# Sums of squares for the FFN's norm: six vector adds become six accumulating transfers, and the norm's factor is taken one pair of projections later

## The chip, the cores and the metric

The kernel runs on one core of a Trainium2 chip. The metric is the device time of one launch in microseconds. A core has a matrix engine (TensorE, PE in the profile, with its weight loads as PEld), a vector engine (VectorE, DVE), an activation engine (ScalarE, ACT), a general engine (GpSimd, POOL) and a queue engine that issues most transfers (SyncE, SP). Each engine takes its own instructions in order; an instruction that must wait holds everything behind it on that engine. Work is handed from one engine to another, and from transfers to engines, by semaphores.

## The reference, cut to what matters

One layer of a streaming encoder on 640 tokens (512 of a prompt, 8 x 16 of samples), model width 1024, in float32. The last two steps of the layer are the ones that matter here:

```
y   = merged @ w_out
h   = x + y                                        # after the mixing part
hn  = h * rsqrt(mean(h*h) + eps) * norm_ffn_g      # RMSNorm over the 1024 channels
a   = silu(hn @ ffn_w_gate) * (hn @ ffn_w_up)      # width 2816
out = h + a @ ffn_w_down                           # then a last RMSNorm
```

The mean of squares is one number for each token. It is a factor that is the same for all channels, so the product with the gate's weights can be formed before it is known and scaled behind it.

## The kernel before, in words

Everything is kept transposed: channels on the 128 partitions, the 640 tokens along the row. A tensor of 1024 channels is four blocks of 256 channels, each a tile of 128 x 2 x 640 (two groups of 128 channels, `m` = 0 and 1). Matrix work goes in jobs, one for each block of 256 output channels, and two jobs make a pair. A job multiplies by seven products instead of eight (a scheme on 2 x 2 blocks whose operands are sums of weight blocks and sums of input blocks, named 1 to 7 in the code); each product is 12 matmuls of 128 x 320 columns for each job, as float32 is split into a high and a low part, `h` and `l`, and three of the four part products are taken. So a pair is 7 x 24 matmuls. The order of the products is 5, 1, 6, 3, 7, 2, 4 in the first pair of a stage (`FIRST`) and 5, 2, 1, 6, 3, 7, 4 in the others (`LATER`). After each product ACT or DVE takes the result out of PSUM (`ev_form`, `ev_add`).

Weights come through one-deep and two-deep staging tiles `wr`. Plain quarters are loaded from SP (L1048). Two of the seven weight operands need a sum of two quarters; there the second quarter is added by an accumulating transfer from POOL (L1051). ACT then casts the high part (`wh`, L90) and DVE subtracts it (`wl`, L85); some operands need one more DVE add first (L1033). This runs up to three products ahead of the matmuls, in four buffers (`HB`).

The stage around the change is the end of the output projection (four `out_job`s, two pairs) and the start of gate and up (eleven pairs, `gu_jobs(0)` to `gu_jobs(10)`: the gate's job and the up's job of one block). When a block j of `h` is complete, `done` writes it to memory (`hspill`), and `squares` squares it in place on ACT (L1561) and adds its two groups into `s`, which is the tile `rbc` (L1563 for block 0, L1566 for blocks 1 to 3: six adds of 128 x 640 on DVE). Blocks 0 and 1 do this at once; those of blocks 2 and 3 wait in the list `late`, and hooks in the first gate/up pair call them after its products 6 and 3. After product 7 of that pair `stats` runs: ten rows of matmul against a column of ones give the sums over partitions (`ptr`, L66), DVE and POOL turn them into the factor (L159, L161), `replicate` spreads it over the partitions (L177 on DVE, two matmuls into `ppv`, ACT copies back into `rbc`, L184). `swiglu(j)` is called when the up's job of pair j has its last product: it scales the gate by `rbc` (L1583), takes tanh on ACT (L1587), two more DVE instructions (L1588, L1589), and writes the result to memory (`aspill`, from SP). The finished blocks are read back (`raw<-aspill`) as input of the down projection while gate and up still run.

The code states a program order; a scheduler then places each engine's instructions, so that neighbours in the code may stand elsewhere in the queue. The tiles `h`, `g`, `u` and `th` share five buffers (`pair`) that go round: a new tile waits until the last reader of the old one is done.

Of the kernel before, what the change touches and what calls it, by code (L numbers as in the profile page):

```python
# [14 lines left out]
ALU = mybir.AluOpType  # L15
# [42 lines left out]
class Builder:  # L58
# [1169 lines left out]
    def post(self):  # L1228

        nc, a = self.nc, self.a  # L1230
# [17 lines left out]
        for j in range(4):  # L1248
            for m in range(2):
                r = raws[j][:, m, :]  # L1250
                nc.vector.scalar_tensor_tensor(r, r, self.g(G_MIX + 2 * j + m), self.rbc, op0=ALU.mult, op1=ALU.mult)
                t = (E, O)[m]
# [37 lines left out]
        for hf in range(2):  # L1290
# [28 lines left out]
            if hf:  # L1319

                h, l = P["w"][5] = flat("wh", F32R), flat("wl", F32R)
# [73 lines left out]
        pairs = [(x, self.LATER) for x in jobs]  # L1395

        def hook(job, p, f, when="post"):
            job.setdefault(when, {}).setdefault(p, []).append(f)
# [55 lines left out]
        def add(jobs):  # L1454
            for i in range(0, len(jobs), 2):
                pairs.append((jobs[i:i + 2], self.LATER if i else self.FIRST))
# [77 lines left out]
        s = self.rbc  # L1534
        late = []

        def out_job(j):
            st = {}

            def load():  # L1540
                if j == 0:
                    sh["t"] = self.ap.tile([128, 4, 2, T], F32, tag="acc", bufs=1, name="hg")
                st["h"] = pair("h")
                self.dma(st["h"], a["xT"][256 * j:256 * j + 256, :].rearrange("(m p) t -> p m t", p=128))
                st["ev"] = self.ev_add(st["h"], done)

            def done(q):
                m, n = q
                h = st["h"]
                ns = slice(HN * n, HN * n + HN)  # L1550
                nc.scalar.activation(sh["t"][:, j, m, ns], h[:, m, ns], AF.Copy, scale=self.g(G_FFN + 2 * j + m))
                if q == (1, 0):
                    self.dma(self.hdram[j], h)
                    if j < 2:
                        squares()
                    else:
                        late.append(squares)

            def squares():
                h = st["h"]  # L1560
                nc.scalar.activation(h, h, AF.Square)  # L1561
                if j == 0:
                    nc.vector.tensor_tensor(s, h[:, 0, :], h[:, 1, :], op=ALU.add)  # L1563
                else:
                    for m in range(2):
                        nc.vector.tensor_tensor(s, s, h[:, m, :], op=ALU.add)  # L1566
            return {"ap": a["w_o"][j], "xc": xo, "ev": lambda p, ps: st["ev"](p, ps), "load": load}

        out = [out_job(j) for j in range(4)]
# [11 lines left out]
        def swiglu(j, g, u):  # L1581
            rb = self.rbc[:, None, :].broadcast_to([128, 2, T])
            nc.vector.tensor_tensor(g, g, rb, op=ALU.mult)  # L1583
            if j >= 8:
                nc.vector.tensor_tensor(u, u, rb, op=ALU.mult)
            th = pair("th")
            nc.scalar.activation(th, g, AF.Tanh, scale=0.5)  # L1587
            nc.vector.scalar_tensor_tensor(g, th, 1.0, g, op0=ALU.add, op1=ALU.mult)  # L1588
            nc.vector.tensor_tensor(g, g, u, op=ALU.mult)  # L1589
            self.dma(self.adram[j], g)  # L1590

        def gu_jobs(j):
            st = {}

            def done(name):
                def f(t, q):
                    st[name] = t
                    if name == "u" and q == (1, 0):
                        swiglu(j, st["g"], t)
                return f  # L1600
            return [{"ap": a["w_fg"][j], "xc": xf, "ev": self.ev_form(lambda: pair("g"), done("g"))},
                    {"ap": a["w_fu"][j], "xc": xf, "ev": self.ev_form(lambda: pair("u"), done("u"))}]

        n0 = len(pairs)
        add([x for j in range(NF // 2) for x in gu_jobs(j)])
        for p in (6, 3):
            hook(pairs[n0][0][1], p, lambda: late.pop(0)())
        hook(pairs[n0][0][1], 7, stats)

        ys = {}  # L1610

# [36 lines left out]
        for j in range(3):  # L1648
            self.dma(raw[:, j], self.adram[8 + j])
            for m in range(2):  # L1650
                h, l = places.pop(0)
# [181 lines left out]
```

## Time and profile before

| | us |
|---|---|
| median of 3 runs | 1284.82 (1284.57 to 1285.51) |
| the profiled execution | 1284.68 |
| its span, first to last instruction | 1282.6 |
| PE busy | 1249.0 (97%) |
| DVE busy | 930.9 (73%) |
| ACT busy | 653.2 (51%) |
| POOL busy | 162.8 (13%) |

The profile is of one execution; 2.1 us of its time lie outside the span. PE is busy 97% of the span, so its idle times are few and each can be looked up with the instruction that ended it. The stage of the change lies between about 820 and 890 us: block 0 of `h` is squared at 825 us, the factor's matmuls stand at 868 us, and the second gate/up pair begins at 877 us. Times in rows are microseconds from the span's start, and an instruction's row gives its start, its duration, its engine, its line and its tiles.

### The profile page before, as it was taken

The numbers are of one execution on the slowest core, as the hardware profiler recorded it, in microseconds if no ns is written. First come the engines' busy times: TensorE is split into PE (matmuls) and PEld (weight loads), VectorE is DVE, ScalarE is ACT, GpSimd is POOL, SyncE is SP. The second block draws the span as 40 slices with busy tenths as digits, with TensorE's granted clock in tenths as the row PEclk, the third lists the DMA queues.
The fourth block names the chain that finished last, engine by engine and source line by source line (L and its number), as shares of the span: only waits on it lengthen the run. The fifth ranks groups of instructions, "written<-read, shape, count | busy, mean of one in ns | idle before, by whom it ended". The sixth has DMA issues, their size and how long they took to land. (4 is left out here: it accounts for less than half of the span.)

```text
span 1282.6 us, 21826 instructions
## 1 busy us (share of the span) xinstructions
PE 1249.0 (97%) x8464; PEld 1197.9 (93%) x8464; DVE 930.9 (73%) x1467; ACT 653.2 (51%) x1135; POOL 162.8 (13%) x190
## 2 busy tenths in 40 slices
PE   7999999999999999999999899999999999999997
PEld 6999899998889779999999899999999999999997
DVE  7844465327777948777779877897777667899975
ACT  6733342326665568645565523574444444656334
POOL 5300001000001401211111001112111211111001
PEclk9999999999999999999999999999999999999998
DMA  7874533353434925876888996668766766697444
GB/s 246 263 275 172 188 111 109 120 169 98 117 103 139 319 40 155 229 198 173 264 267 253 295 338 192 174 174 229 192 185 186 186 166 171 183 248 203 128 133 132
DMA packets 107415, 241.21 MB, mean 188 GB/s; under 512 B 11120, under 2 KB 21232, under 8 KB 107312
## 3 DMA queue, kind: packets, MB, share of 16 engines
q1 hardware_dynamic: 89680, 204.43, 48.3%
q0 software_dynamic: 17360, 35.14, 14.4%
q8 instruction: 66, 1.08, 0.3%
q14 instruction: 37, 0.30, 0.1%
q10 hardware_dynamic: 272, 0.26, 0.1%
HBM read 204.50 MB, written 34.24 MB: 186 GB/s over the span
## 5 line engine op out<-in xcount | busy, mean ns | idle before, releaser
L85 DVE TENSOR_TENSOR wl<-wr,wh 128x1024 fp32r<-128x1024 f32 (+5 forms) x325 | 332.5, 1035 | 142.9 <-ACT wh L90 140.8
L90 ACT CAST wh<-wr 128x1024 fp32r<-128x1024 f32 (+5 forms) x325 | 281.7, 881 | 237.0 <-PE psX L1111 82.7
L1111 PE MATMUL psX<-Eh,wl 128*128 128x320 f32 x304 | 95.9, 315 | 3.3 <-DVE g L1137 3.3
L1111 PE MATMUL psX<-El,wh 128*128 128x320 f32 x304 | 94.5, 311 | 0.0
L1111 PE MATMUL psX<-Eh,wh 128*128 128x320 f32 x304 | 94.5, 311 | 0.0
L1033 DVE TENSOR_TENSOR wr<-wr 128x1024 f32<-128x1024 f32 x52 | 63.5, 1220 | 0.3
L1111 PEld LDWEIGHTS psX<-Eh,wl 128*128 128x128 f32 x304 | 57.7, 190 | 4.5 <-DVE g L1137 3.8
L1111 PE MATMUL psX<-c,wh 128*128 128x320 f32 x272 | 60.1, 309 | 0.0
L1111 PEld LDWEIGHTS psX<-Eh,wh 128*128 128x128 f32 x304 | 57.9, 190 | 0.2 <-issue 0.2
L1111 PEld LDWEIGHTS psX<-El,wh 128*128 128x128 f32 x304 | 57.7, 190 | 0.0
L66 PE MATMUL psb<-xh,wl 128*128 128x320 f32 x224 | 53.4, 319 | 0.0
L196 ACT ACTIVATE P<-psc,nb 128x256 f32<-128x256 f32 (+4 forms) x60 | 30.3, 506 | 44.0 <-DVE nb L190 38.5
L66 PE MATMUL psb<-xl,wh 128*128 128x320 f32 x224 | 51.5, 311 | 0.0
L66 PE MATMUL psb<-xh,wh 128*128 128x320 f32 x224 | 50.8, 308 | 0.0
L1051 POOL DMA_DIRECT2D wr<-in_w_fg x22 | 19.6, 892 | 243.3 <-DVE wl L85 122.7
L1111 PE MATMUL psZ<-Oh,wl 128*128 128x320 f32 x152 | 47.4, 312 | 1.0 <-DVE wl L85 1.0
L190 DVE TENSOR_REDUCE nb<-psc 128x1 f32<-128x256 f32 (+4 forms) x60 | 27.0, 456 | 27.6 <-PE psc L66 27.0
L1111 PE MATMUL psZ<-Ol,wh 128*128 128x320 f32 x152 | 47.0, 309 | 0.0
L1111 PE MATMUL psZ<-Oh,wh 128*128 128x320 f32 x152 | 46.9, 309 | 0.0
L1111 PEld LDWEIGHTS psX<-c,wh 128*128 128x128 f32 x272 | 45.5, 188 | 0.0
L1111 PE MATMUL psX<-c,wl 128*128 128x320 f32 x136 | 42.2, 310 | 0.6 <-DVE h L1151 0.5
L66 PEld LDWEIGHTS psb<-xh,wl 128*128 128x128 f32 x224 | 36.2, 188 | 5.9 <-issue 5.8
(507 smaller groups left out, 4068.5 us busy)
## 6 DMA issues: line engine op xcount, KB each, us to landing
wr<-in_w_fg SPq DMA_DIRECT2D x55, 256.0 KB, 3.7
wr<-in_w_fu SPq DMA_DIRECT2D x55, 256.0 KB, 4.4
wr<-in_w_fd SPq DMA_DIRECT2D x40, 256.0 KB, 4.2
cache<-in_ck SPq DMA_DIRECT2D x8, 1024.0 KB, 8.5
cache<-in_cv SPq DMA_DIRECT2D x8, 1024.0 KB, 7.7
aspill<-g SPq DMA_DIRECT2D x11, 640.0 KB, 3.2
raw<-aspill SPq DMA_DIRECT2D x11, 640.0 KB, 7.6
wr<-in_w_ft SPq DMA_DIRECT2D x16, 384.0 KB, 3.0
```

Source lines behind the costliest of these rows:

```text
L66: i = self.nc.tensor.matmul(out, lhsT=l, rhs=r, start=start, stop=stop)
L85: self.keep(self.nc.vector.tensor_tensor(out, a, b, op=ALU.subtract))
L90: self.keep(self.nc.scalar.copy(h, src))
L190: nc.vector.reduce_max(nb, ps, axis=AX.X, negate=True)
L196: nc.scalar.activation(P, ps, AF.Exp, bias=nb, scale=scale, accum_out=se)
L1033: nc.vector.tensor_tensor(src, src, r[{6: "11", 3: "12"}[p]], op=ALU.add)
L1051: self.nc.gpsimd.dma_start(out=t[:, 512 * k:512 * k + 512], in_=part(job, self.QUARTERS.index("22" if q == "s1" else "11")), accum_op=ALU.add)
L1111: self.nc.tensor.matmul(ps, lhsT=lw[:, ws], rhs=rx[:, k, :], start=first and k == 0 and i == 0, stop=last and k == 3 and i == 2, skip_grou ...
```

## The change

Three things differ. The six DVE adds at L1566 become six transfers from POOL that add `h` into `rbc` in place (`accum_op`); block 0 keeps its DVE add. The squares of blocks 2 and 3 are called after products 5 and 1 of the first gate/up pair instead of 6 and 3. The factor (`stats`) is taken after product 5 of the gate's job of the second pair instead of after product 7 of the first, and `swiglu(0)` is put off until after product 5 of the up's job of the second pair.

```diff
                 else:
                     for m in range(2):
-                        nc.vector.tensor_tensor(s, s, h[:, m, :], op=ALU.add)
+                        nc.gpsimd.dma_start(out=s, in_=h[:, m, :], accum_op=ALU.add)
...
                     if name == "u" and q == (1, 0):
-                        swiglu(j, st["g"], t)
+                        if j:
+                            swiglu(j, st["g"], t)
+                        else:
+                            late.append(lambda: swiglu(0, st["g"], t))
...
         n0 = len(pairs)
         add([x for j in range(NF // 2) for x in gu_jobs(j)])
-        for p in (6, 3):
+        for p in (5, 1):
             hook(pairs[n0][0][1], p, lambda: late.pop(0)())
-        hook(pairs[n0][0][1], 7, stats)
+        hook(pairs[n0 + 1][0][0], 5, stats)
+        hook(pairs[n0 + 1][0][1], 5, lambda: late.pop(0)())
```

The first place to look at is POOL's queue from the weights of the first gate/up pair on. In the names, `wr_9053` is a staging tile of the first gate/up pair, `wr_9516` (now `wr_9492`) the tile for product 5 of the third pair and `wr_9295` (now `wr_9298`) that for product 7 of the second; `fg` and `fu` are the gate's and the up's weights. Before:

```order
L1051 DMA wr_9053<-in_w_fg 128x512
L1051 DMA wr_9053<-in_w_fu 128x512
L1051 DMA wr_9516<-in_w_fg 128x512
L1051 DMA wr_9516<-in_w_fu 128x512
L1051 DMA wr_9295<-in_w_fg 128x512
L1051 DMA wr_9295<-in_w_fu 128x512
L161 TENSOR_TENSOR rstd_9438<-ms_9436,mhalf_73 128x5
```

And now, where `h_8873` is block 2 and `h_8889` is block 3:

```order
L1051 DMA wr_9053<-in_w_fg 128x512
L1051 DMA wr_9053<-in_w_fu 128x512
L1566 DMA rbc_74<-h_8873 128x640 x2
L1566 DMA rbc_74<-h_8889 128x640
L1051 DMA wr_9492<-in_w_fg 128x512
L1051 DMA wr_9492<-in_w_fu 128x512
L1051 DMA wr_9298<-in_w_fg 128x512
L1051 DMA wr_9298<-in_w_fu 128x512
L1566 DMA rbc_74<-h_8889 128x640
L161 TENSOR_TENSOR rstd_9528<-ms_9526,mhalf_73 128x5
```

Three of the four adds of blocks 2 and 3 stand ahead of the four weight transfers, and the last stands behind them. Since all write `rbc`, each add waits on POOL until the one ahead of it has landed. The two adds of block 1 stand further up, ahead of the tile for product 5 of the second pair.

The second place is PE's queue at the factor's matmuls (`ptr`). Before, they stand in the first pair, inside the gate's product 2 (`psZ_9452`):

```order
L1111 MATMUL psZ_9452<-Ol_4956,wh_9328 128x320
L1111 MATMUL psZ_9452<-Oh_4955,wl_9329 128x320
L1111 MATMUL psZ_9452<-Oh_4955,wh_9328 128x320
L66 MATMUL ptr_9430<-ones_71,rbc_74 128x1 x5
L1111 MATMUL psZ_9452<-Ol_4956,wh_9328 128x320
L1111 MATMUL psZ_9452<-Oh_4955,wl_9329 128x320
```

Now they stand between the two jobs of the second pair's product 5 (`psY_9505` is the gate's, `psY_9538` the up's):

```order
L1111 MATMUL psY_9505<-c6h_4957,wl_9401 128x320
L1111 MATMUL psY_9505<-c6h_4957,wh_9400 128x320
L1111 MATMUL psY_9505<-c6l_4958,wh_9400 128x320
L66 MATMUL ptr_9520<-ones_71,rbc_74 128x1 x5
L1111 MATMUL psY_9538<-c6h_4957,wl_9401 128x320
L1111 MATMUL psY_9538<-c6h_4957,wh_9400 128x320
```

They have moved back by the rest of the first pair and by 12 matmuls of the second, and they now wait for the landing of the last add, where before they waited for DVE.

On ACT both late squares now stand ahead of the cast for product 3 of the first pair, where before the second of them stood four casts further down. On DVE the six adds are gone; `swiglu(0)` stays in the second pair, some instructions later.

## Rows read from the trace of the kernel before

**Rows 1.** The page's first part: busy time of each engine.
```profile
PE 1249.0 (97%) x8464; PEld 1197.9 (93%) x8464; DVE 930.9 (73%) x1467; ACT 653.2 (51%) x1135; POOL 162.8 (13%) x190
```

**Rows 2.** Stretches of 10 us: PE, PEld, DVE, ACT, POOL busy; clock, DMA share, GB/s.
```profile
830.00:840.00 10.00, 9.59 (x66) 9.33 (x65) 9.64 (x16) 6.79 (x10) 3.36 (x4) 1.00 0.64 182
840.00:850.00 10.00, 9.82 (x67) 9.56 (x67) 10.00 (x13) 5.79 (x9) 0.17 (x1) 1.00 0.75 168
850.00:860.00 10.00, 8.17 (x54) 7.64 (x53) 9.88 (x14) 8.97 (x15) 0.00 (x0) 1.00 0.38 152
860.00:870.00 10.00, 9.77 (x69) 9.77 (x70) 9.01 (x14) 5.17 (x6) 3.94 (x5) 1.00 0.81 211
```

**Rows 3.** PE's timeline: matmuls behind idle time (in brackets: idle us and its releaser).
```profile
736.45 0.42 PE L1111 MATMUL psX<-Oh,wl 128*128 128x320 f32 x1 [3.07 <-DVE g L1137]
...
860.23 0.41 PE L1111 MATMUL psY<-c7h,wl 128*128 128x320 f32 x1 [1.52 <-DVE wl L85]
...
924.17 0.41 PE L1111 MATMUL psX<-Eh,wl 128*128 128x320 f32 x1 [1.47 <-DVE g L1137]
```

**Rows 4.** Line 1566: the six adds, ns min/median/max, first and last start.
```profile
L1566 DVE TENSOR_TENSOR rbc<-rbc,h x6: 817/821/825, 829.4 to 866.9; 128x640 f32<-128x640 f32 x6
```

**Rows 5.** ACT's timeline at the squares of blocks 2 and 3.
```profile
855.55 1.28 ACT L1561 ACTIVATE h<-h 128x1280 f32<-128x1280 f32 x1
...
857.67 2.95 ACT L90 CAST wh<-wr 128x1024 fp32r<-128x1024 f32 x3
...
861.78 1.29 ACT L1561 ACTIVATE h<-h 128x1280 f32<-128x1280 f32 x1
```

**Rows 6.** SP's timeline at the writes of blocks 2 and 3.
```profile
851.37 0.80 SPq L77 DMA_DIRECT2D hspill<-h  x2
```

**Rows 7.** The page's part 6, transfers: count, KB each, median us to landing.
```profile
hspill<-h SPq DMA_DIRECT2D x4, 640.0 KB, 4.1
```

**Rows 8.** POOL's timeline at the weights that stand behind the new adds.
```profile
863.87 0.86 POOL L1051 DMA_DIRECT2D wr<-in_w_fg  x1 [23.69 <-DMA wr<-in_w_fg]
...
867.24 1.14 POOL L1051 DMA_DIRECT2D wr<-in_w_fu  x1
```

**Rows 9.** Line 1051, all accumulating weight transfers of the trace: us to landing.
```profile
DMA to landing us min/median/max: 3.9/7.5/11.5
```

**Rows 10.** The same line, its four transfers between 860 and 875 us.
```profile
DMA to landing us min/median/max: 7.4/9.3/10.0
```

**Rows 11.** Stretches of 2 us, same columns as rows 2.
```profile
858.00:860.00 2.00, 0.71 (x5) 0.45 (x4) 2.00 (x3) 2.00 (x3) 0.00 (x0) 1.00 0.00 0
...
862.00:864.00 2.00, 2.00 (x15) 2.00 (x15) 2.00 (x3) 1.07 (x1) 0.13 (x1) 1.00 1.03 291
```

**Rows 12.** The chain of waits at the factor's matmuls: start, us, what.
```profile
868.28 1.01 PE ptr L66 x10
...
872.19 0.86 PE ppv L66 x2
...
873.93 0.37 PE ppv L66 x2
...
876.94 3.52 PE psY L1111 x24
```

**Rows 13.** The chain of waits from 955 to 985 us.
```profile
975.79 5.32 PE psX L1111 x24
```

**Rows 14.** Stretches around that place and behind the longest idle time of rows 3.
```profile
736.00:740.00 4.00, 3.55 (x24) 3.55 (x25) 4.00 (x6) 0.44 (x1) 0.00 (x0) 1.00 0.93 296
...
976.00:978.00 2.00, 2.00 (x13) 2.00 (x12) 1.97 (x4) 0.64 (x1) 0.00 (x0) 0.80 0.42 78
978.00:980.00 2.00, 2.00 (x9) 2.00 (x9) 2.00 (x2) 0.53 (x2) 0.00 (x0) 0.50 0.05 15
```

**Rows 15.** DVE's timeline at the first gate's scaling.
```profile
875.69 1.49 DVE L1583 TENSOR_TENSOR g<-g,rbc 128x1280 f32<-128x1280 f32 x1 [0.70 <-ACT g L1135]
```

**Rows 16.** ACT's timeline in the third pair: a cast of the down projection's input.
```profile
920.78 0.73 ACT L90 CAST Oh<-raw 128x640 fp32r<-128x640 f32 x1 [3.70 <-DMA raw<-aspill]
```

## The prediction

> **What bounds the kernel now.** I read the page's busy times first: PE is busy 1249.0 of 1282.6 us [rows 1], so the time is PE's work plus its idle times, and a change is worth what it does to these. Then the stretches of 10 us around the change: from 830 to 870 us PE is idle 0.41, 0.18, 1.83 and 0.23 us, together 2.65 us, and DVE is busy 38.5 of the 40 us [rows 2]. Then PE's timeline: the largest of these, 1.52 us at 860.23, ended with a DVE instruction, the low part of a weight [rows 3]. So in this stage DVE makes PE wait, and the reader sees at once the most that can be won there: 2.65 us, 0.2% of the time. Last I read the queues that the new work goes to: POOL's timeline, the landing times of its transfers, and the place of the factor's matmuls in PE's queue.
>
> **The change part by part.** *Removed:* six DVE adds of 0.82 us [rows 4], 4.9 us of DVE's time in the stretch where it is full. Two lie before 832 us, four between 858 and 868 us. By the first two DVE can be 1.6 us early when block 3 of h is complete.
>
> *The squares, moved.* Each is 1.28 us on ACT. Before, the square of block 2 started at 855.55 us and the three casts behind it at 857.67; the square of block 3 came behind those, at 861.78 [rows 5]. A square overwrites h, so it waits for h's write to memory: issued at 851.37 [rows 6], landing after a median 4.1 us [rows 7], at 855.5. With DVE up to 1.6 us early the write goes out at about 850.0 and lands at 854.1, so I put the square of block 2 at 854.1 to 855.4 and that of block 3, behind two short copies, at 855.9 to 857.1. The cast of product 3's weight comes behind both: 1.0 us on ACT and 1.2 us on DVE, so PE can start that product at 859.3 instead of 860.23 [rows 3]. That is a gain of 0.9 us, not 1.52: the squares take back part of what DVE gives. Bounds: 2.65 us won, if every idle time of the stretch goes, and 0.7 lost, if the write lands at 855.5 as before.
>
> *Moved on PE:* the ten rows at the factor's sums, 1.01 us, and the matmuls that spread it, 0.86 and 0.37 [rows 12], 2.24 us in all. They are moved, not saved. Product 5 of the second pair started at 876.94 and takes 3.52 us for both jobs [rows 12]. The new place is behind the gate's half, at 876.94 + 1.76 = 878.70; without the 2.24 us that no longer stand ahead PE is there at 876.46, and at 875.6 with the 0.9 us won.
>
> *Added: a chain of waits.* Each add into rbc waits until the one ahead has landed, so the four adds of blocks 2 and 3 are a chain from the square of block 2, at 855.4, to the factor's matmuls. The adds of block 1 start at 828.5 and have landed before that at any of the durations below; they delay the transfers behind them by 1 to 3 us, which lie over ten us ahead of their use. The trace before has no add from one tile on the chip to another. The nearest rows are the accumulating transfers of weights, 256 KB against 320 KB here: 3.9 us to landing at least, 7.5 median [rows 9], and in the very stretch, between 860 and 875 us, 7.4 at least and 10.0 at most [rows 10]. From both sides:
> - Low: 3.9 us each. The third add is issued at 855.4 + 7.8 = 863.2, so the weights behind it keep their times, 863.87 to 867.24 plus 1.14 [rows 8]; the last add follows at 868.4 and lands at 872.3. PE does not wait.
> - High: 10.0 us each: 855.4 + 40 = 895.4. PE waits from 875.6 on, almost 20 us.
>
> I take it step by step. The first add meets idle transfer engines (share 0.00 from 858 to 860 us) [rows 11]: close to the least, 4.6 us with a quarter more bytes, landing at 860.0. The second and third run while the weights of the next pairs come in (share 1.03) [rows 11]; the 7.4 to 10.0 us of that stretch are of transfers issued in pairs, and these go alone, so I take 6.5 us each: 866.6 and 873.1. The four weight transfers are issued from 867.7 on, behind the third add. The last add is issued at 873.2, and in its own queue about 1 MB of weights stands ahead of it. Before, that megabyte took from 863.87 to at most 867.24 + 10.0 = 877.2, 13.4 us [rows 8, 10], which from 867.7 is 881.1. The last add can't be much earlier than its forerunners: I put its landing at 881. PE, at its place since 875.6, stands for 5.4 us. What was won before that is lost in this wait: against the old order the end moves by 881 - 876.5 = 4.5 us.
>
> By the Trainium skill this would come out otherwise. "DMA: Bandwidth & Descriptors", section "Anatomy of one DMA — SWDGE (gpsimd) path", fits a transfer from POOL as 2.0 us plus its bytes at 436 GB/s: 2.75 us for 320 KB as an estimate, so that the last add would land at 868.4 + 2.75 = 871.2 and PE would not wait at all. The trace does not agree: no accumulating transfer in it landed in under 3.9 us, and the median is twice that [rows 9]. Its case is the second rival below.
>
> *The clock.* Behind an idle time that ended at 975.79, the granted clock was 0.80 and then 0.50 for some 3 us [rows 14], and 24 matmuls took 5.32 us instead of 3.52 [rows 13, 12]. Behind the idle times of 1.47, 1.52 and 3.07 us of rows 3 nothing such is seen; from 736 to 740 us the clock was 1.00 [rows 14]. So the cost of a stop is 0 to 1.8 us. As the stop I forecast is longer than any of these, I take the loss less the slow start, 1.6 us.
>
> *At nothing:* swiglu(0) put off. Its first instruction started at 875.69 [rows 15], so its 4.5 us of DVE lay in the second pair anyway, where DVE has room. If that cover fails, the copy of product 1 behind it delays product 6 by a few tenths up to 2 us. The transfers behind the late `aspill` on SP are weights due 20 us later. In the third pair ACT waits 3.70 us for an input of the down projection [rows 16], which gives PE's 1.47 us at 924.17 [rows 3]; that transfer hangs on pair 1's swiglu, which moves with PE, so I leave it (bounds: all 1.47 won, 1.5 lost).
>
> **Sum.** 1284.68 (the profiled execution) + 4.5 + 1.6 = 1290.8 us. The median of the runs is 0.14 above that execution, which is within their spread.
>
> **The rivals.**
> 1. *The weights ahead of the last add drain faster, and the stop is short.* The last add lands near 877, as the weights did before. For it: POOL has idle time, and part of the transfers from SP that filled the stretch come at other times now. Against it: the third add cannot land before the weights are issued unless the adds are as short as the least. Then PE waits 0.5 to 3 us, with no clock loss: 876.5 to 878.5 against 876.5, so 1284.7 to 1286.7, about 1285.7.
> 2. *The chain is covered* (faster). If the last add has landed by 875, the place of the factor's matmuls costs nothing and the change keeps its gain: 0.9 to 2.65 us, with up to 1.47 in the third pair. It decides at 4.5 us or less for each of the first three adds, and a last add that does not queue behind the weights. Time 1284.68 - 2.5 = 1282.2. For it: the least row and the skill's fit; against it: the busy stretch.
> 3. *The adds are as slow as the weights of that stretch*, 9.3 us each [rows 10]: 855.4 + 37.2 = 892.6, PE stands 17 us, and the end moves by 16.1 + 1.6: 1302.4. Against it: those come in pairs, on a full queue.
>
> **How the numbers follow.** A measurement of this kernel can tell about 0.2%, 2.6 us, from no change. Forecast (a stop that costs 2.6 to 11 us): 0.60. Rival 3 and what lies between (over 11 us): 0.10. Rival 1, within 2.6 us: 0.21. Rival 2, faster by more than 2.6 us, or by its smaller gains with luck in the third pair: 0.09. So slower 0.70, same 0.21, faster 0.09. The forecast's own range is 1287.3 to 1295.5. The range for 8 in 10 takes in rival 1 and leaves out most of rivals 2 and 3: 1283.5 to 1297.
>
> **What the profile would show.** Line 1566 among POOL's transfers with six of 320 KB and its time to landing: about 6 us bears out the forecast, under 4.5 rival 2, over 8 rival 3. PE's timeline: the first `ptr` row behind an idle time of about 5 us, released by a transfer into rbc, near 881 us, and a clock below 1.00 behind it. DVE's share from 830 to 870 us a tenth lower, and PE's idle time at product 3 of the first pair smaller by about 1 us. I am wrong if `ptr` has no idle time ahead of it, or if a longer stop stands elsewhere: at a late weight of the second or third pair, or at product 6 behind swiglu(0).

## The result and the profile after

The changed kernel takes 1297.26 us (median of 4 runs, 1294.3 to 1298.7) against 1284.69 us of the kernel before, run beside it (4 runs, 1282.41 to 1285.51): a ratio of 1.0096, 95% interval 1.0078 to 1.0114. It is slower by 12.6 us, where 6.1 had been forecast; 0.26 us above the top of the range, 1297. The profiled execution took 1296.63 us, of them 1294.7 in the span.

The busy times of the engines answer to [rows 1]:

```profile
PE 1252.6 (97%) x8464; PEld 1201.2 (93%) x8464; DVE 926.7 (72%) x1461; ACT 652.0 (50%) x1135; POOL 169.0 (13%) x196
```

DVE has six instructions less and POOL six more, so the adds did become transfers. PE is busy 3.6 us longer, with the same number of matmuls: some of them ran at a lower clock, as the stretches at the end of this section show.

PE's timeline, the matmuls behind the largest idle times from 700 to 1000 us, answers to [rows 3]:

```profile
736.72 0.63 PE L1111 MATMUL psX<-Oh,wl 128*128 128x320 f32 x1 [3.17 <-DVE g L1137]
...
858.12 0.41 PE L1111 MATMUL psX<-c5h,wl 128*128 128x320 f32 x1 [1.44 <-ACT g L1132]
...
887.74 2.27 PE L66 MATMUL ptr<-ones,rbc 128*128 128x1 f32 x10 [9.81 <-DMA rbc<-h]
...
938.25 0.42 PE L1111 MATMUL psX<-Eh,wl 128*128 128x320 f32 x1 [1.34 <-DVE g L1137]
...
989.45 0.41 PE L1111 MATMUL psX<-Eh,wl 128*128 128x320 f32 x1 [1.43 <-DVE g L1137]
```

One stop is new, and it is the large one: 9.81 us ahead of the factor's first matmul, ended by a transfer into rbc. The others stand where they stood before. The stop at product 3 of the first pair, 1.52 us in [rows 3], is gone, but 1.44 us stand at product 6, one product earlier, instead.

The stretches of 10 us answer to [rows 2], same columns:

```profile
830.00:840.00 10.00, 9.42 (x64) 9.09 (x63) 10.00 (x15) 7.98 (x11) 2.67 (x4) 1.00 0.67 159
840.00:850.00 10.00, 10.00 (x70) 9.99 (x69) 9.82 (x15) 6.87 (x11) 2.56 (x3) 1.00 1.03 225
850.00:860.00 10.00, 8.56 (x59) 8.30 (x58) 9.30 (x13) 8.46 (x15) 0.86 (x1) 1.00 0.54 195
860.00:870.00 10.00, 10.00 (x69) 9.83 (x69) 8.69 (x10) 5.04 (x7) 0.86 (x1) 1.00 0.78 179
```

PE's idle time here is 0.58 + 0 + 1.44 + 0 = 2.02 us, against 2.65. That the relief of DVE wins so little is seen on ACT's timeline around the squares [rows 5]:

```profile
856.49 1.27 ACT L1561 ACTIVATE h<-h 128x1280 f32<-128x1280 f32 x1
857.65 0.41 ACT L1132 COPY g<-psX 128x320 f32<-128x320 f32 x1
857.96 0.43 ACT L1132 COPY u<-psX 128x320 f32<-128x320 f32 x1
858.27 1.29 ACT L1561 ACTIVATE h<-h 128x1280 f32<-128x1280 f32 x1
859.45 2.94 ACT L90 CAST wh<-wr 128x1024 fp32r<-128x1024 f32 x3
```

The square of block 2 stands ahead of the two copies that empty psX, and PE's product 6 waits for the first of these. What DVE no longer delays, ACT does.

POOL's timeline shows the new transfers, rbc<-h, among the weights, wr, that were in [rows 8]:

```profile
858.04 0.86 POOL L1566 DMA_DIRECT2D rbc<-h  x1 [13.96 <-ACT h L1561]
863.47 0.86 POOL L1566 DMA_DIRECT2D rbc<-h  x1 [4.56 <-DMA rbc<-h]
871.73 0.86 POOL L1566 DMA_DIRECT2D rbc<-h  x1 [7.40 <-DMA rbc<-h]
872.27 1.22 POOL L1051 DMA_DIRECT2D wr<-in_w_fg  x1
872.80 1.58 POOL L1051 DMA_DIRECT2D wr<-in_w_fu  x1
873.37 1.90 POOL L1051 DMA_DIRECT2D wr<-in_w_fg  x1
873.91 2.25 POOL L1051 DMA_DIRECT2D wr<-in_w_fu  x1
875.71 1.34 POOL L1566 DMA_DIRECT2D rbc<-h  x1
```

The chain of waits from there on, start, us and what, says how long each took and who waited; its last two rows answer to [rows 12]:

```profile
858.04 4.87 DMA rbc<-h
...
863.47 7.73 DMA rbc<-h
...
875.71 11.90 DMA rbc<-h
887.60 0.14 issue
887.74 2.27 PE ptr L66 x10
890.00 3.14 PE psY L1111 x12
```

The first add needs 4.87 us to land, the second 7.73, the third 3.7 (the least of the six, below), the last, issued behind four weights, 11.90. PE came to its place at 877.93 (887.74 less 9.81) and stood until that landed. Line 1566's landing time, all six:

```profile
DMA to landing us min/median/max: 3.7/6.3/11.9
```

Last TensorE's granted clock (1.00 is 2.4 GHz, 0.50 the lower level of 1.2 GHz), the number behind the busy times, in stretches of 2 us at the untouched place around 736 us and behind the new stop [rows 14]:

```profile
736.00:738.00 2.00, 1.28 (x5) 1.28 (x6) 2.00 (x5) 0.00 (x0) 0.00 (x0) 0.50 0.91 250
738.00:740.00 2.00, 2.00 (x9) 2.00 (x9) 1.67 (x2) 0.00 (x0) 0.00 (x0) 0.50 0.95 386
...
888.00:890.00 2.00, 2.00 (x11) 2.00 (x10) 0.00 (x0) 0.00 (x0) 0.00 (x0) 0.50 0.04 8
...
892.00:894.00 2.00, 2.00 (x13) 2.00 (x12) 0.82 (x1) 0.82 (x2) 0.40 (x1) 0.83 0.72 220
```

Behind the stop the ten rows of sums take 2.27 us instead of 1.01, and twelve matmuls 3.14 instead of 1.76. But the clock was also low behind 736 us, in code that the change does not touch, where it was 1.00 before. The two profiled executions, place by place (when PE came to the same place, after less before, and what was added since the row above; the factor's place is 877.93 against the 876.46 that the prediction works out for the old order):

| place | after less before, us | added | by |
|---|---|---|---|
| 736 us, ahead of the change | 0.27 | 0.27 | |
| 811 us, still ahead of it | 2.50 | 2.23 | clock 0.50 behind 736 us |
| PE at the factor's place | 1.47 | -1.03 | DVE's relief |
| `ptr` | 11.28 | 9.81 | the stop |
| ahead of PE's stop at the end of the third pair, 922.70 us before | 14.21 | 2.93 | clock 0.50 behind the stop |
| 981 us before, end of the fifth pair | 12.37 | -1.84 | two stops 0.13 and 0.41 shorter; 1.29 by the clock, which was low behind the second before and not after |
| end of the span | 12.1 | -0.27 | |

The change itself makes -1.03 + 9.81 + 2.93 = 11.71 us; the rest is the clock in unchanged code, up in one place and down in another.

### The profile page after: what moved, and what is told of

The parts are those of the page before. It is cut to its first block, busy times and chain, and to the rows that moved or that the text cites. A ratio compares the mean times of both kernels' runs of the same rounds, so it can differ in the third digit from the quotient of the medians.

```text
span 1294.7 us, 21841 instructions
## 1 busy us (share of the span) xinstructions
PE 1252.6 (97%) x8464; PEld 1201.2 (93%) x8464; DVE 926.7 (72%) x1461; ACT 652.0 (50%) x1135; POOL 169.0 (13%) x196
## 4 chain that ended last, share of the span: by engine, by line
PE 38%; DMA 6%; DVE 3%; ACT 2%; issue 1%; POOL 0%; SPq 0%; POOLq 0%; ACTq 0%; DVEq 0%
PE psX L1111 20%; PE psY L1111 10%; PE psZ L1111 5%; PE psb L66 3%; DMA rbc<-h 2%; DVE wl L85 2%; DMA raw<-aspill 1%; ACT wh L90 1%; DMA wr<-in_w_o 1%; DMA wr<-in_w_g_mem 1%; DMA wr<-in_w_br_gm 0%; DMA hspill<-h 0%; DMA wr<-in_w_ft 0%; PE ptr L66 0%; POOL wr L1051 0%
```

## The experiments

What had to be told apart: whether the transfers make the stop or the moved calls do (theories A and C); if the transfers, whether it is the last one's place behind the weights (A1) or the chain of four as such (A2); and whether the clock around 736 us belongs to the change (D says no). The first four kernels ran on one chip, with 25 runs of the kernel before beside them (median 1284.68 us); the last three on another. Each trace is of a single execution, which can lie some us from the median of its kernel; where it does, this is said.

**The adds back on DVE, the calls where the change put them.**

```diff
-                        nc.gpsimd.dma_start(out=s, in_=h[:, m, :], accum_op=ALU.add)
+                        nc.vector.tensor_tensor(s, s, h[:, m, :], op=ALU.add)
```

> The changed kernel with the six adds back on DVE; the new hooks stay (squares behind products 5 and 1, factor and first gate in the second pair). Theory A (the whole loss is the wait of the factor's first matmul for the last add from POOL, 9.81 us, and the low clock behind it, about 3 us): no idle time ahead of ptr, 1283 to 1286 us. Theory C (the moved hooks cost the time, by the late first gate or the late squares): still over 1290 us without any wait for a transfer into rbc.

1286.17 us (10 runs), ratio 1.0013, interval 0.9998 to 1.0029; 0.17 us above what theory A gave. PE's timeline has no idle time ahead of `ptr`; the largest near it is at product 3:

```profile
862.74 0.41 PE L1111 MATMUL psY<-c7h,wl 128*128 128x320 f32 x1 [2.38 <-DVE wl L85]
```

So the moved calls by themselves cost at most 0.3% (the top of the interval), and nothing that can be told from none. The late swiglu(0) makes PE wait nowhere near it: from 863 to 905 us PE's largest idle time is 0.36 us. The 2.38 us at product 3, against 1.52 in [rows 3], go with both squares standing ahead of its cast while DVE still has its adds.

**The transfers alone, the calls where they were before.**

```diff
 (of the kernel before)
-                        nc.vector.tensor_tensor(s, s, h[:, m, :], op=ALU.add)
+                        nc.gpsimd.dma_start(out=s, in_=h[:, m, :], accum_op=ALU.add)
```

> The kernel before with its adds of blocks 1 to 3 as transfers from POOL; hooks as before, so the factor's matmuls stand in the first pair, some 7 us of PE's work earlier than in the changed kernel. Theory A: the chain of adds ends at about the same time (885 to 888 us), PE waits for it 15 to 18 us, and the time is 1300 to 1304 us: the later place of the factor pays for part of the adds. Theory C: no worse than 1292 us, as the old hooks are back.

1300.85 us (4 runs), ratio 1.0137, interval 1.0114 to 1.0160. The chain of waits:

```profile
854.38 3.62 DMA rbc<-h
858.56 7.66 DMA rbc<-h
866.76 5.05 DMA rbc<-h
872.09 8.06 DMA rbc<-h
880.29 2.27 PE ptr L66 x10
```

The stop is 12.99 us, from 867.30 (880.29 less that); 15 to 18 had been expected, as the chain ended at 880.15 and not between 885 and 888, while the time came out as expected. The loss comes with the transfers: without the moved calls it is larger, since PE comes to the factor's place some 8 us sooner (867.30, against 877.93 less the 2.5 us by which that trace lags ahead of the change). The durations repeat: a short first one, a long second one, a last one that ends about 13 us after the first of the four weights behind the third (issued at 867.29; landing at 880.15), in the changed kernel 15 (872.27; 887.60).

**The last add ahead of the four weights.** The weights are held in program order behind the adds of blocks 2 and 3; both squares are called at product 5. PE, DVE, ACT and SP keep the order of the changed kernel: in the two traces their instructions follow one another alike, and on POOL one add alone has moved.

```diff
-                        nc.gpsimd.dma_start(out=s, in_=h[:, m, :], accum_op=ALU.add)
+                        i = nc.gpsimd.dma_start(out=s, in_=h[:, m, :], accum_op=ALU.add)
+                        j > 1 and (setattr(self, "pinw", True), self.tc.keep_in_program_order(i))
...
-        for p in (5, 1):
+        for p in (5, 5):
 (and the weights' transfers: self.pinw and self.tc.keep_in_program_order(i), until the factor is taken)
```

> The changed kernel with one difference: on POOL the last add stands ahead of the four weight transfers instead of behind them; PE, DVE, ACT and SP have the same rows in the same order. Theory A1 (the last add's 11.9 us to landing are the megabyte of weights ahead of it in POOL's queue): it is issued when the third has landed, at about 876 us, lands 4 to 6 us later, PE waits 2 to 4.5 us instead of 9.81, and the time is 1288 to 1291 us. Theory A2 (adds from one tile on the chip to another are slow by themselves while the transfers from SP run, whatever stands ahead of them): the last add still takes over 9 us, PE waits over 7 us, over 1293 us.

1288.13 us (10 runs), ratio 1.0035, interval 1.0016 to 1.0053. POOL's timeline:

```profile
868.06 0.86 POOL L1567 DMA_DIRECT2D rbc<-h  x1 [6.72 <-DMA rbc<-h]
872.23 0.86 POOL L1567 DMA_DIRECT2D rbc<-h  x1 [3.31 <-DVE u L1140]
872.85 1.13 POOL L1051 DMA_DIRECT2D wr<-in_w_fg  x1
```

and the chain of waits:

```profile
860.47 7.05 DMA rbc<-h
868.06 3.63 DMA rbc<-h
872.23 4.66 DMA rbc<-h
877.01 1.25 PE ptr L66 x10
```

The same transfer of 320 KB lands in 4.66 us with nothing ahead of it in its queue, against 11.90. PE waits 1.90 us instead of 9.81, and the clock is low only from 878 to 882 us. The ratio falls from 1.0096 to 1.0035, some 8 us of 1285: A1 holds for the last add. What A2 says of adds beside SP's transfers is seen on the second one alone, 7.05 us.

An obvious rival is SP's queue: in the changed kernel SP issues two weights and one more transfer of 320 KB just behind the last add (876.22 to 877.12, 0.5 to 1.4 us later). It issues the same three here, 0.9 to 1.8 us behind it (873.13 to 874.00), and POOL its four weights as well (872.85 to 874.46). So SP's transfers and the weights beside the add do not make the 11.90 us by themselves; what differs is that the weights stand ahead of it there and behind it here.

This trace is of an execution of 1284.58 us, 3.55 us below the median of its kernel and no longer than the kernel before. It shows what the order does to the stop; whether longer stops or a lower clock make the 3.45 us by which the median lies above the kernel before, no trace shows.

**The factor later, the order of the transfers left alone.**

```diff
-        hook(pairs[n0 + 1][0][0], 5, stats)
-        hook(pairs[n0 + 1][0][1], 5, lambda: late.pop(0)())
+        hook(pairs[n0 + 1][0][1], 1, stats)
+        hook(pairs[n0 + 1][0][1], 6, lambda: late.pop(0)())
```

> The changed kernel with the factor taken later: behind product 1 of the up's job of the second pair (48 matmuls, 7.0 us of PE's work later), the first gate behind product 6. Theory A: the chain of adds lands at the same time, 887 to 888 us, and the wait shrinks by the 7.0 us to about 2.8 us, with or without the low clock: 1287 to 1290 us. Theory C: a later first gate costs more, over 1297 us.

1285.67 us (10 runs), ratio 1.0015, interval 0.9998 to 1.0032, where theory A gave 1287 to 1290. The trace is of an execution of 1288.65 us. PE's timeline:

```profile
886.35 1.25 PE L66 MATMUL ptr<-ones,rbc 128*128 128x1 f32 x10 [1.09 <-DMA rbc<-h]
...
892.31 1.10 PE L66 MATMUL ppv<-tmp,ones 128*128 128x512 f32 x2 [2.85 <-DVE tmp L177]
```

The last add still takes 11.4 us, but lies beside matmuls, and the stop is 1.09 us (2.8 had been expected). A second one stands at the matmuls that spread the factor, and POOL's timeline has part of its cause:

```profile
888.34 0.86 POOL L1051 DMA_DIRECT2D wr<-in_w_fg  x1 [12.22 <-DMA wr<-in_w_fg]
888.88 1.22 POOL L1051 DMA_DIRECT2D wr<-in_w_fu  x1
889.44 1.87 POOL L161 TENSOR_TENSOR rstd<-ms,mhalf 128x5 f32<-128x5 f32 x1
```

The factor's own small POOL instruction comes behind the issue of two weights. The other part is the place: only 12 matmuls stand between `ptr` and `ppv` here, 1.86 us, where the kernel before had 19, 2.90 us from the end of `ptr` to `ppv` in [rows 12].

**Both: adds first, and the factor a little later** (than in the third kernel).

```diff
-        hook(pairs[n0 + 1][0][0], 5, stats)
-        hook(pairs[n0 + 1][0][1], 5, lambda: late.pop(0)())
+        hook(pairs[n0 + 1][0][0], 2, stats)
+        hook(pairs[n0 + 1][0][1], 1, lambda: late.pop(0)())
```

> The adds-first kernel with the factor behind product 2 of the gate's job of the second pair, 24 matmuls or 3.5 us of PE's work later, and the first gate behind product 1 of the up's job. Theory A1: the last add lands before PE comes to ptr, so no idle time there, and what DVE gives between 830 and 870 us stays: PE's idle times there 1.4 instead of 2.66 us, time 0 to 3 us under the kernel before in runs with the same clock, 1281 to 1285 us. Rival: the later first gate meets the second pair's own gate on DVE and PE waits 1 us or more in the second or third pair, which eats the gain.

1285.77 us (12 runs) against 1285.39 of the kernel before (17 runs): ratio 1.0001, interval 0.9985 to 1.0017; 1281 to 1285 had been expected. The trace is of the longest of the 12, 1289.30 us. No stop had been expected; 1.43 us were left in it, since the second add, issued at 864.78, held up the third until 873.41 and the last took longer than in the third kernel:

```profile
873.41 3.62 DMA rbc<-h
877.56 5.87 DMA rbc<-h
```

PE's idle time from 830 to 870 us is 2.29 us, not the 1.4 expected: the 1.44 us at product 6 stand here too. The rival's stops in the third pair are not borne out: the one there is 1.66 us, at the place where the kernel before has 1.47 [rows 3]. So with most of the loss taken out, the change is worth nothing that can be measured; what the first pair gave in the changed kernel is about 1 us, less than executions of one kernel differ by.

**The kernel before again**, word for word, for its clock.

> The kernel before, word for word, in another execution. Theory D (what differs between runs of one kernel is whether the clock falls behind the same idle times): PE's idle times of 3.1 us near 736 and 1.5 to 1.9 us near 924 and 976 stand where they stood, and a clock below 1.00 stands behind one of them, another one or none; the time follows, 1.5 to 2.5 us for each. Rival: the idle times themselves differ by as much as the runs do.

A single execution, 1284.70 us. PE's timeline at the untouched place:

```profile
736.63 0.42 PE L1111 MATMUL psX<-Oh,wl 128*128 128x320 f32 x1 [3.50 <-DVE g L1137]
```

The stretch of 2 us behind that stop:

```profile
738.00:740.00 2.00, 2.00 (x10) 2.00 (x9) 2.00 (x3) 0.44 (x1) 0.00 (x0) 0.52 1.01 399
```

The stop around 736 us was now followed by a clock of 0.52, as in the changed kernel, and the one at 976 us was not, unlike [rows 14]. So this part of the difference is no doing of the change. The rival holds as well: the stops themselves differ between executions of this kernel, 3.50 against 3.07 us here and 1.23 against 1.84 at 976 us.

**The changed kernel again**, word for word.

> The changed kernel, word for word, in another execution. Theory A: the wait ahead of ptr is 8 to 11 us again, with the last add 10 to 12 us to landing behind four weight transfers; theory D: near 736 us the clock may stay at 1.00 this time, and the span is then about 2.3 us shorter than that of the first execution's 1294.7.

A single execution, 1292.09 us. PE's timeline:

```profile
734.65 0.42 PE L1111 MATMUL psX<-Oh,wl 128*128 128x320 f32 x1 [1.30 <-DVE g L1137]
...
882.40 1.84 PE L66 MATMUL ptr<-ones,rbc 128*128 128x1 f32 x8 [9.04 <-DMA rbc<-h]
```

The stop at the factor is there again, 9.04 us, with a last add of 10.96 us. The stop around 736 us was 1.30 us this time, with the clock at 1.00 behind it, and the execution is 4.5 us shorter than the first, where 2.3 had been expected of the clock alone. All of that was won ahead of the factor: PE came to its place at 873.36 (882.40 less 9.04), 4.57 us earlier than in the first.

## Why the prediction was right and wrong

*What bounds the kernel, and the size of the gain:* right in the number, by luck in how. 1.03 us came back where 0.9 had been forecast, and product 3 started at 861.81, 859.3 when the 2.5 us by which this trace lags ahead of the change are taken off, just as forecast. But its own stop went altogether, and another of 1.44 us came at product 6, which waits for a copy on ACT behind the square of block 2. That square began at 856.49, 854.0 less the same 2.5 us, against 854.1 forecast. The reason given, that it waits for h's write, did not hold it: the write issued at 852.56 had landed after 2.9 us, at 855.46, and ACT was at its casts until the square began.

*The chain of waits and where it ends:* right at its ends, in part by luck. Forecast and found, the found ones less the same 2.5 us: first add issued at 855.4 and 855.5; last add issued at 873.2 and 873.2; PE at its place at 875.6 and 875.4. The single durations were off in ways that cancelled: 4.6, 6.5 and 6.5 us had been put down; 4.87, 7.73 and 3.7 were found, with about 0.5 us of hand-over behind the first and the second, for which nothing had been put down.

*The landing of the last add:* this is the step that failed. "I put its landing at 881", that is 7.8 us behind its issue; it took 11.90, and 10.96, 11.4 and 8.06 in the other runs that keep the order. Less the 2.5 us it landed at 885.1, 4.1 us late. Half of that is the megabyte of weights that stands ahead of it: it was to be issued from 867.7 on and was from 869.8, since the second add and the hand-overs took longer than put down. The other half is behind the weights. The landing times of the four, in the trace of after:

```profile
DMA to landing us min/median/max: 5.9/8.2/11.3
```

The 11.3 is the last one's: issued at 873.91, it landed at 885.2. So the megabyte took 12.9 us from the first issue (872.27), about the 13.4 that the working took. But the add has 320 KB of its own to move behind it, and nothing was put down for these: it landed 2.4 us after the last weight, and 2.4, 2.3 and 1.6 us after it in the same other runs. With all this the stop was 9.81 us instead of 5.4. The mechanism, a transfer that queues behind the weights, was the right one, as the third experiment shows: without them ahead 4.66 us.

*The clock:* right in kind, too small. 1.6 us had been put down after the 24 matmuls of [rows 13]; 2.93 us were lost behind the stop, where the clock was at its lower level until 892.7 us, 1.26 of them at the sums themselves (2.27 against 1.01), which were the first to meet the low clock.

*The sum:* 4.5 + 1.6 = 6.1 us forecast, 11.71 found in the steps of the change. The 12.6 us between the medians hold the clock of unchanged places besides, which differs from execution to execution. They fall among the times over 11 us, to which 0.10 had been given, though the third rival's mechanism, every add at 9.3 us, was not found. One slip hangs on nothing else: 11 us above 1284.68 is 1295.7, not the 1295.5 at which the forecast's own range ends.

*The second rival*, a covered chain, failed on the second (7.73 us) and the last add (11.90), and narrowly on the first (4.87, where it asked for 4.5). Beside it stood the fit of the Trainium skill ("DMA: Bandwidth & Descriptors", section "Anatomy of one DMA — SWDGE (gpsimd) path"), 2.75 us as an estimate. No run here shows it: the shortest of these adds took 3.6 us. The Trainium skill says in the same page ("DMA: Bandwidth & Descriptors"), section "Queues, rings and completion order", that a DMA engine takes turns between the queues that have work for it; that fits block 2's second add of 7.0 to 8.1 us in every kernel with the transfers, in a stretch in which SP's weights come in, but no run here took those away. Of the 7.2 us between 4.66 and 11.90 it is also open how much the add waits for its turn in POOL's queue and how much for transfer engines that the weights ahead keep busy: the third experiment takes both away at once.

## What to carry to other kernels

Work that is moved from an engine to a transfer leaves a full engine for a full queue: look at what will stand ahead of the last transfer in its own queue, and add its own bytes to what these need. Where the engine that bounds the kernel waits for the last of a chain, the order of issue can be worth more than the instructions saved; here it made some 8 us of 12.6, the saved DVE work about 1. A number that comes out right does not show that its reason was: here two errors cancelled in the chain. And the gain that a change can make in a stage is bounded by the idle time there before it: 2.65 us could never have been more than 0.2%.

## What the runs showed of the hardware

- An accumulating transfer of 320 KB between two tiles on the chip landed in 3.6 to 5.9 us where it was the first or the third of its chain, or the last with no weights ahead of it; in 7.0 to 8.5 as the second of block 2 and of block 1 alike; in 8.1 to 11.9 behind four weight transfers of POOL's queue.
- Four weights issued from POOL one right behind the other have rows of 1.22, 1.58, 1.90 and 2.25 us, against 0.86 for one by itself; they start 0.5 us apart all the same.
- The same stop of PE, at the same place of unchanged code, was followed by a clock of 1.00 in one execution (3.07 us) and of 0.50 in another (3.17 us). The low clock made 2.23 us there, so it has to be subtracted before a change of this size is explained. The length of the stop does not tell which it will be: at this place 3.24 us (third experiment) left the clock at 1.00, while 2.84 (fourth) and 2.98 (fifth) were followed by 0.50.
